# A two-layer hybrid attention and MLP trunk on one core: attention's matmuls in a fixed order, q and k stacked by transfers, weight loads on another queue

## The chip, the core and the metric

The kernel runs on one core of one Trainium2 chip. Its matrix engine (TensorE, PE in the profile) multiplies; VectorE (DVE) and ScalarE (ACT) do elementwise work; GpSimd (POOL) does little here; SyncE (SP) issues transfers. The time is the device time of one execution in microseconds (us), smaller is better; a kernel's time is the median over its runs.

## The reference

Sequence 512, width 1024, two layers, all in float32. Each layer has an attention part and a gated MLP part, both conditioned on a vector c by modulations (scale, shift, gate). The attention has sixteen heads in three groups: four heads A (differential attention: two score maps per head, rotary), six heads B (a mixture of dilated windows, rotary), six heads C (a data-dependent bias from cumulative log-forget gates).

```python
h = rmsnorm(x) * (1 + scale1(c)) + shift1(c)
qa, ka, va, qb, kb, vb, qc, kc, vc, fz = split(h @ w_in)
oa = softmax(qa1 ka1') va - lam * softmax(qa2 ka2') va      # A, rotary q and k
ob = dilated-window mixture over rotary qb, kb, vb          # B
oc = softmax(qc kc' + cum[q] - cum[k]) vc                   # C, cum = cumsum(log_sigmoid(fz + bias))
x = x + gate1(c) * (concat(oa, ob, oc) @ w_out)
x = x + gate2(c) * MLP(rmsnorm(x) * (1 + scale2(c)) + shift2(c))
```

## The kernel before

Products keep float32's precision by splitting each operand into a high and a low part of a type that PE multiplies in one pass; one product is three matmuls (hi by hi, low by hi, hi by low), issued by mm3 (L250 to L253). A weight tile arrives by a 512 KB load (L148, tile raww, three buffers), ACT makes its high part (L174, whi), DVE the low part (L186, wlo). Modulations are also loaded by 512 KB tiles (L214, rawm, two buffers) and reduced on DVE (L217); they are spread over the attention loops and the MLP.

A framework builds the program: it takes the operations in the order in which the code issues them as a priority and sets for each engine an order of its own, with waits between the engines; an operation may be passed by a later one of its engine that the framework expects to be ready sooner. issue_after keeps one operation behind another.

layer_attn (L366) works on eight head pairs, ORDER = B0 B1 A0 C0 A1 C1 B2 C2, indexed 0 to 7. Each pair has eight blocks: two heads by four blocks of 128 queries; the n-th query block sees the first 128 n keys. The loop at L806 runs over all 64 blocks. For block b it issues the scores of the next block (emit_S, L611: tile s in PSUM), the masked row maximum on DVE (L641), the exponential on ACT (L654), and for the block two back (lag = 2) the transposes (L682, tile pt), the high part on ACT (L701, pth), the low part on DVE (L706, ptl) and the product with V (emit_PV, L728 and L729, tile po). Between these steps fill (L590) spends a budget on other PE work of the pair: the next pair's q and k projections (qk_chunk, L494: 24 matmuls a side into a PSUM tile qkps), then half of a group of V products (v_half, L388: 48 matmuls of 256 columns, tile vps), and for the last pair the first output products (out_part, tile ops).

A projection is followed by qk_post (L446), one step at a time between blocks. For A and B: ACT copies the PSUM tile (L456), two transfers swap even and odd rows (L458, L459, on SP), DVE applies the rotary tables (L462, L464, L466). Then the operands of the scores are laid out so that one 128-row matmul holds two of the three split products:

- B and C: stack_gen (L416) builds stacked tiles qk from half-height (64-row) steps: high part on ACT (L423), low part on DVE (L420), copies on ACT (L434, L436). For C it reads the projection's PSUM tile itself, which stays occupied so long.
- A: one high and one low part (split_gen, L240 and L242), then twelve transfers of 32 rows for each side (L477).
- C gets its bias as four extra rows (L443), which come from fz_post (L508): a chain of small DVE operations on z, two sums on PE (pf, L536 and L537), transposes (pa, L559).

PSUM has eight banks: three of the pool mm (projections, V and output products), two for s, two for pt, one for po. Weight and modulation loads, swaps and layout transfers all go out on SP's queue, in one order.

Of the kernel before, what the change touches and what calls it, by code (L numbers as in the profile page):

```python
# [30 lines left out]
def kernel(  # L31
# [106 lines left out]
    class Weights:  # L138
        def __init__(self):
            self.raw, self.w = {}, {}  # L140
            self.nd = self.nh = self.nl = self.nu = 0
            self.pt = None

        def dma(self, upto):
            while self.nd < min(upto, len(plan)):
                src, n, at = plan[self.nd]
                t = rawp.tile([128, 4 * VZ], F32, tag="raw", name="raww")
                nc.sync.dma_start(out=t[:, 0:n], in_=src)  # L148
                self.raw[self.nd] = t
                self.nd += 1  # L150

# [93 lines left out]
    def pair_tiles(pool, tag, name):  # L245
        hi = pool.tile([128, SEQ], F32R, tag=tag, name=name + "h")
        lo = pool.tile([128, SEQ], F32R, tag=tag, name=name + "l")
        return hi, lo

    def mm3(ps, w, rhs, first, last, c=slice(0, SEQ)):  # L250
        T.matmul(ps[:, c], w[0], rhs[0][:, c], start=first, stop=False, skip_group_check=True)  # L251
        T.matmul(ps[:, c], w[0], rhs[1][:, c], start=False, stop=False, skip_group_check=True)  # L252
        T.matmul(ps[:, c], w[1], rhs[0][:, c], start=False, stop=last, skip_group_check=True)  # L253

    def feat_q(ps, w, act, first=True, last=True, k0=0):
        n = len(act)
# [109 lines left out]
    def layer_attn(l, ap, mods, st, rt0):  # L366
# [21 lines left out]
        def v_half(q, half):  # L388
            nb, n = (1, VZ) if q == 0 else (2, 256)
            if half == 0:  # L390
                pools = {"m": (mm, "mm"), "t": (ps_t, "pt"), "o": (ps_o, "o")}
                vps[q] = [pools[c][0].tile([128, SEQ], F32, tag=pools[c][1], name="vps")
                          for c in ("otmt" if q == 0 else "mm")]
            pss = vps[q]
            w = W.use()
            for j in range(4):
                k = 4 * half + j
                wc = w(n * j, n * j + n)
                for tb in range(4):
# [4 lines left out]
                    T.matmul(d, h[k][0][:, b], wc[0], start=go, stop=False, skip_group_check=True)  # L404
                    T.matmul(d, h[k][0][:, b], wc[1], start=False, stop=False, skip_group_check=True)
                    T.matmul(d, h[k][1][:, b], wc[0], start=False, stop=en, skip_group_check=True)
                W.pump(j)
                yield
            if half == 1:
                if q == 0:  # L410
                    for tb in range(4):
                        V.tensor_tensor(out=z[:, tb, :], in0=pss[tb][:, 256:VZ], in1=fb[:, l, :], op=ALU.add)
                vvs[q] = ap.tile([128, 4, 4, 128], F32R, tag="vv", name="vv", bufs=2)
                aux.append(v_post(q, lambda tb: pss[tb // nb][:, 256 * (tb % nb):256 * (tb % nb) + 256]))

        def stack_gen(src, side, res, pair=None):  # L416
            R = (H0, H1)

            def sub(out, h):
                V.tensor_tensor(out=out, in0=src[R[h]], in1=res[h][R[h]].bitcast(F32), op=ALU.subtract)  # L420

            for h in range(2):
                A.activation(out=res[h][R[h]], in_=src[R[h]], func=AF.Copy)  # L423
                yield
                if side == 0:
                    sub(res[h][R[1 - h]], h)
                elif pair is None:
                    sub(res[2 + h][R[h]], h)
                else:
                    sub(res[2 + h][H0], h)  # L430
                yield
                dup = res[h][R[1 - h]] if side == 1 else res[2 + h][H0] if pair is not None else None
                if dup is not None:
                    A.activation(out=dup, in_=src[R[h]], func=AF.Copy)  # L434
                if side == 1 and pair is None:
                    A.activation(out=res[2 + h][R[1 - h]], in_=res[2 + h][R[h]].bitcast(F32), func=AF.Copy)  # L436
                yield
            if pair is not None:
                while not aug:
                    yield  # L440
                for h in range(2):
                    c = 24 * side + 4 * (2 * (pair - 5) + h)
                    nc.sync.dma_start(out=res[2 + h][64:68, :].bitcast(F32), in_=aug[0][c:c + 4, :].bitcast(F32))  # L443
                yield

        def qk_post(idx, side, ps, kind):  # L446
# [1 line left out]
            res = [ap.tile([128, SEQ], F32R, tag="qk", name="qk", bufs=QKB) for _ in range(n)]  # L448
            qks[idx, side] = res
            if kind == "C":  # L450
                yield from stack_gen(ps, side, res, ORDER[idx][1])
                qkdone.add((idx, side))
                return
            tb = rope_tile(kind)
# [11 lines left out]
            V.tensor_tensor(out=qf, in0=qf, in1=sw, op=ALU.add)  # L466
            yield
            if kind != "A":
                yield from stack_gen(qf, side, res)
# [98 lines left out]
        def out_part(m):  # L568
            ops[m] = mm.tile([128, SEQ], F32, tag="mm", name="ops") if m < 3 else ps_s.tile([128, SEQ], F32, tag="s", name="ops")
            w = W.use()  # L570
            for k in range(7):
# [3 lines left out]
                W.pump(k)  # L575
                yield

        fills = []
        for idx in range(8):
            f = []  # L580
# [6 lines left out]
            cost = (10.4 if idx < 7 else 9.08) + (5.2 if idx < 6 else 0)  # L587
            fills.append([f, cost, 0.0])

        def fill(idx, share):  # L590
# [20 lines left out]
        def emit_S(b):  # L611
# [3 lines left out]
            qb = slice(128 * i, 128 * i + 128)  # L615
            if kind != "A":
                s = ps_s.tile([128, SEQ], F32, tag="s", name="s")
                T.matmul(s[:, 0:n], q[hh][:, qb], k[hh][:, 0:n], start=True, stop=False)
                if kind == "B":
                    T.matmul(s[:, 0:n], q[hh][:, qb], k[2 + hh][:, 0:n], start=False, stop=True)  # L620
                else:
                    T.matmul(s[:, 0:n], q[2 + hh][0:68, qb], k[2 + hh][0:68, 0:n], start=False, stop=True)
                S[b] = [s]
                return
            res = []
            for mp in range(2):
                s = ps_s.tile([128, SEQ], F32, tag="s", name="s")
                T.matmul(s[:, 0:n], q[2 * hh + mp][0:96, qb], k[2 * hh + mp][0:96, 0:n], start=True, stop=True)  # L628
                res.append(s)
            S[b] = res  # L630

# [41 lines left out]
        def emit_T(b):  # L673
# [5 lines left out]
                pt = ps_t.tile([128, SEQ], F32, tag="pt", name="pt")  # L679
            for j in range(i + 1):  # L680
                c = 128 * (i + j) if i < 2 else 128 * j
                T.transpose(pt[:, c:c + 128], e[:, 128 * j:128 * j + 128], ident)  # L682
# [25 lines left out]
        def emit_PV(b):  # L708
# [14 lines left out]
            for j in range(nj):  # L723
# [4 lines left out]
                T.matmul(po[:, oc], vv[:, j, hd, :], pth[:, pc], start=(j == 0), stop=False, skip_group_check=True)  # L728
                T.matmul(po[:, oc], vv[:, j, hd, :], ptl[:, pc], start=False, stop=(j == nj - 1), skip_group_check=True)  # L729
            if half == 1:  # L730
                aux.append(head_post(idx, kind, hh, po))

# [69 lines left out]

        emit_S(0)
        lag = 2
        f1, f2, f3 = 0.06, 0.055, 0.055
        for b in range(nb + lag):  # L806
            idx = blocks[min(b, nb - 1)][0]
            while idx and fills[idx - 1][0]:
                fill(idx - 1, 1.0)
            p = b - lag  # L810
# [13 lines left out]
            if p >= 0:  # L824
                emit_hi(p)
            fill(idx, f1)
            if b < nb:
                emit_exp(b)
            if p >= 0:
                emit_lo(p)  # L830
            fill(idx, f2)
            if b + 1 < nb:
# [2 lines left out]
            if b < nb:  # L835
                emit_norm(b)
            fill(idx, f3)
            if p >= 0:
# [6 lines left out]
        for idx in range(8):  # L845
            while fills[idx][0]:
                fill(idx, 1.0)
        while any(g.__name__ == "head_post" for g in aux):
# [332 lines left out]
```

## Time and profile before

| | |
|---|---|
| median of 3 runs | 1338.02 us (1337.93 to 1339.64) |
| the profiled execution | 1334.63 us |
| its span | 1332.9 us |
| PE, DVE, ACT busy in the span | 96%, 64%, 48% |
| mean granted PE clock | 0.989 |
| attention loop, first layer | about 64 to 283 us |
| attention loop, second layer | about 716 to 927 us |

The median stands 3.4 us above the profiled execution, whose time is 1.7 us longer than the span. In the profile a row names the line, the engine, the operation and the program's tiles, out<-in; busy time and the mean of one; and the idle time of the engine ahead of it with what ended it. A PE row is a matmul whose end is modelled, and rows overlap, so PE's idle time shows only gaps that are longer than that overlap.

### The profile page before, as it was taken

To read this page: it belongs to the slowest core of one execution; us is meant where nothing else is said; L and a number is where in the kernel's file an instruction comes from. 1 tells how busy PE (TensorE), PEld (TensorE's weight loads), DVE (VectorE), ACT (ScalarE), POOL (GpSimd) and SP (SyncE) were. 2 spreads that over 40 slices of the span, in tenths; PEclk is the share of its full clock that TensorE was granted. 3 is DMA by queue.
4 is the path that set the end of the run, shared out by engine and by line. 5 is a ranking of instruction groups with operands and counts; after the bars stand their busy time and mean duration, and the time that the engine had idled before them with its cause. 6 is when DMAs were issued, how large, how long until landed. Compare 5 with 4: busy or idle time off the path is not lost.

```text
span 1332.9 us, 17722 instructions
## 1 busy us (share of the span) xinstructions
PE 1277.8 (96%) x6568; PEld 1058.6 (79%) x6568; DVE 858.2 (64%) x1600; ACT 642.3 (48%) x1158; POOL 22.9 (2%) x16
## 2 busy tenths in 40 slices
PE   4899999999999999999999999999999999999997
PEld 1788888788877778888898888878878888888886
DVE  6888999868888874423347788875754444443232
ACT  5576677745333243322336677785543333333231
POOL 5100000000000000000000000000000000000000
PEclk8899999999999999999999999999999999999999
DMA  9345454433888853332432334212133333332331
GB/s 373 140 141 183 152 180 136 130 110 129 269 261 266 267 173 95 91 103 87 117 110 95 90 103 141 66 56 90 48 109 96 97 95 95 95 91 87 103 99 63
DMA packets 56601, 174.39 MB, mean 131 GB/s; under 512 B 8130, under 2 KB 10450, under 8 KB 56516
## 3 DMA queue, kind: packets, MB, share of 16 engines
q1 hardware_dynamic: 55364, 172.16, 41.0%
q8 instruction: 52, 0.85, 0.3%
q10 hardware_dynamic: 1088, 1.05, 0.2%
q14 instruction: 33, 0.27, 0.1%
q0 software_dynamic: 64, 0.06, 0.0%
HBM read 159.41 MB, written 2.10 MB: 121 GB/s over the span
## 4 chain that ended last, share of the span: by engine, by line
PE 53%; DMA 8%; DVE 7%; ACT 4%; issue 3%; SPq 0%; DVEq 0%; ACTq 0%
DMA rawm<-in_wmod_dram 7%; PE dps L251 6%; PE dps L253 6%; PE dps L252 6%; PE pu L251 4%; PE pu L253 4%; PE pu L252 4%; PE pg L252 4%; PE pg L253 4%; PE pg L251 4%; DVE wlo L186 1%; DVE rawm L217 1%; PE qkps L251 1%; PE qkps L252 1%; PE qkps L253 1%
## 5 line engine op out<-in xcount | busy, mean ns | idle before, releaser
L186 DVE TENSOR_TENSOR wlo<-raww,whi 128x1024 fp32r<-128x1024 f32 (+3 forms) x188 | 224.2, 1193 | 241.0 <-ACT whi L174 236.5
L174 ACT ACTIVATE whi<-raww 128x1024 fp32r<-128x1024 f32 (+3 forms) x188 | 194.5, 1035 | 329.6 <-PE dps L252 137.7
L253 PE MATMUL pu<-hh,wlo 128*128 128x512 f32 (+1 forms) x368 | 141.2, 384 | 3.5 <-DVE wlo L186 3.5
L252 PE MATMUL pg<-hl,whi 128*128 128x512 f32 (+1 forms) x368 | 143.0, 389 | 1.5 <-DVE hl L300 1.5
L251 PE MATMUL pg<-hh,whi 128*128 128x512 f32 (+1 forms) x368 | 141.6, 385 | 1.6 <-ACT whi L174 1.6
L251 PE MATMUL pu<-hh,whi 128*128 128x512 f32 (+1 forms) x368 | 142.4, 387 | 0.5 <-ACT whi L174 0.5
L253 PE MATMUL pg<-hh,wlo 128*128 128x512 f32 (+1 forms) x368 | 140.9, 383 | 1.1 <-DVE wlo L186 1.1
L252 PE MATMUL pu<-hl,whi 128*128 128x512 f32 (+1 forms) x368 | 140.7, 382 | 0.0
L251 PE MATMUL dps<-mh,whi 128*128 128x512 f32 x308 | 121.5, 395 | 0.0
L253 PE MATMUL dps<-mh,wlo 128*128 128x512 f32 x308 | 121.5, 394 | 0.0
L252 PE MATMUL dps<-ml,whi 128*128 128x512 f32 x308 | 121.2, 393 | 0.0
L217 DVE CUSTOM_DVE_ANT_0 rawm<-rawm,scb,bm 128x1024 f32<-128x1024 f32 x80 | 102.3, 1279 | 23.7 <-DMA rawm<-in_wmod_dram 23.4
L654 ACT ACTIVATE e<-e,nm 128x256 f32<-128x256 f32 (+3 forms) x160 | 89.0, 557 | 33.0 <-DVE nm L641 29.9
L251 PE MATMUL qkps<-hh,whi 128*128 128x512 f32 x224 | 95.1, 424 | 4.7 <-ACT qk L434 4.1
L898 ACT ACTIVATE y<-y 128x512 f32<-128x512 f32 x44 | 27.8, 632 | 142.6 <-DVE y L895 142.6
L252 PE MATMUL qkps<-hl,whi 128*128 128x512 f32 x224 | 89.7, 400 | 0.0
L253 PE MATMUL qkps<-hh,wlo 128*128 128x512 f32 x224 | 89.6, 400 | 0.0
L253 PEld LDWEIGHTS pu<-hh,wlo 128*128 128x128 f32 x368 | 69.1, 188 | 22.1 <-DVE wlo L186 6.9
L641 DVE CUSTOM_DVE_ANT_0 e<-s,cst 128x256 f32<-128x256 f32 (+3 forms) x160 | 76.4, 481 | 12.0 <-PE s L628 3.7
L252 PEld LDWEIGHTS pg<-hl,whi 128*128 128x128 f32 x368 | 69.0, 188 | 17.7 <-DVE hl L300 3.1
L253 PEld LDWEIGHTS pg<-hh,wlo 128*128 128x128 f32 x368 | 69.0, 188 | 16.7 <-DVE wlo L186 1.9
L251 PEld LDWEIGHTS pg<-hh,whi 128*128 128x128 f32 x368 | 69.1, 188 | 16.0 <-ACT whi L174 2.0
(176 smaller groups left out, 2663.2 us busy)
## 6 DMA issues: line engine op xcount, KB each, us to landing
raww<-in_wup_dram SPq DMA_DIRECT2D x88, 512.0 KB
rawm<-in_wmod_dram SPq DMA_DIRECT2D x80, 512.0 KB
raww<-in_wqk_dram SPq DMA_DIRECT2D x32, 512.0 KB
raww<-in_wdown_dram SPq DMA_DIRECT2D x32, 512.0 KB
mu<-in_wmod_dram SPq DMA_DIRECT2D x16, 512.0 KB
raww<-in_wout_dram SPq DMA_DIRECT2D x16, 448.0 KB
raww<-in_wv_dram SPq DMA_DIRECT2D x12, 512.0 KB
raww<-in_wdown_dram SPq DMA_DIRECT2D x16, 384.0 KB
```

The lines of the kernel that those rows point to most:

```text
L174: A.activation(out=h[:, 0:m], in_=self.raw[i][:, c:c + m], func=AF.Copy)
L186: V.tensor_tensor(out=lo[:, 0:m], in0=raw[:, c:c + m], in1=h[:, 0:m].bitcast(F32), op=ALU.subtract)
L217: V.tensor_tensor_reduce(out=raw, in0=raw, in1=scb, scale=1.0, scalar=bm[:, l, ci:ci + 1], op0=ALU.mult, op1=ALU.add, accum_out=dst)
L251: T.matmul(ps[:, c], w[0], rhs[0][:, c], start=first, stop=False, skip_group_check=True)
L252: T.matmul(ps[:, c], w[0], rhs[1][:, c], start=False, stop=False, skip_group_check=True)
L253: T.matmul(ps[:, c], w[1], rhs[0][:, c], start=False, stop=last, skip_group_check=True)
L641: anchor[0] = V.tensor_tensor_reduce(out=e[:, 0:n], in0=s[:, 0:n], in1=cst[:, mask + SEQ - n:mask + SEQ], scale=-scale, scalar=3e38, op0=A ...
L654: anchor[1] = A.activation(out=e[:, 0:n], in_=e[:, 0:n], func=AF.Exp, bias=nm, scale=-1.0, accum_out=den).ins
L898: last_silu[0] = A.activation(out=y, in_=y, func=AF.Silu).ins
```

## The change

Five edits, all for the two attention loops:

1. *Source order on PE.* Every matmul and transpose of the loop goes through a wrapper (pe, mmul) which ties it behind the one issued before it, so that PE's order is the order of the code. The tie is on from behind the first emit_S to the end of the loop. Since mm3's matmuls go through the wrapper, PE's rows of projections, V, scores and PV all stand at one line (L259).
2. *Budgets.* The shares of the fills change from 0.17 in each block to tables (near, far, 0.125) which put more of the projections into a pair's first blocks and the V products into the later ones; two pieces of output products move to pairs 6 and 7. Each block has four more turns for the steps between. PV of a block is issued one block later.
3. *Stacking.* For B and C, split_gen makes one 128-row high part (ACT) and one low part (DVE); the stacked tiles are filled by 64-row transfers on SP (128 KB each): four for B's q, eight for B's k, six for each side of C.
4. *Queue.* In the loop, weight and modulation loads go out on GpSimd's queue in place of SP's.
5. What follows from these: with them the order of the loads and of other operations around the loop moves too.

The core of the difference:

```diff
+            self.q = nc.sync
...
-                nc.sync.dma_start(out=t[:, 0:n], in_=src)
+                self.q.dma_start(out=t[:, 0:n], in_=src)
...
-        nc.sync.dma_start(out=raw, in_=wmod[l, ci])
+        W.q.dma_start(out=raw, in_=wmod[l, ci])
...
+    row = [False, None]
+
+    def pe(ins):
+        with (tc.issue_after(row[1]) if row[0] and row[1] else ExitStack()):
+            r = ins()
+        row[1] = r.ins
+
+    def mmul(*a, **k):
+        pe(lambda: T.matmul(*a, **k))
...
-        def stack_gen(src, side, res, pair=None):
+        def stack_gen(src, hi, lo, side, res, pair=None):
             R = (H0, H1)
-
-            def sub(out, h):
-                V.tensor_tensor(out=out, in0=src[R[h]], in1=res[h][R[h]].bitcast(F32), op=ALU.subtract)
-
+            yield from split_gen(src, hi, lo)
             for h in range(2):
-                A.activation(out=res[h][R[h]], in_=src[R[h]], func=AF.Copy)
-                yield
                 if side == 0:
-                    sub(res[h][R[1 - h]], h)
-                elif pair is None:
-                    sub(res[2 + h][R[h]], h)
+                    cp = [(h, R[h], hi), (h, R[1 - h], lo)] + ([(2 + h, H0, hi)] if pair is not None else [])
                 else:
-                    sub(res[2 + h][H0], h)
-                yield
-                dup = res[h][R[1 - h]] if side == 1 else res[2 + h][H0] if pair is not None else None
-                if dup is not None:
-                    A.activation(out=dup, in_=src[R[h]], func=AF.Copy)
-                if side == 1 and pair is None:
-                    A.activation(out=res[2 + h][R[1 - h]], in_=res[2 + h][R[h]].bitcast(F32), func=AF.Copy)
+                    cp = [(h, H0, hi), (h, H1, hi), (2 + h, H0, lo)] + ([(2 + h, H1, lo)] if pair is None else [])
+                for j, rows, t in cp:
+                    nc.sync.dma_start(out=res[j][rows, :].bitcast(F32), in_=t[R[h], :].bitcast(F32))
                 yield
...
+        near = [0.155, 0.155, 0.15, 0.15, 0.12, 0.1, 0.085, 0.085]
...
+            if idx == 6:
+                f += [part(outs[0], 6)]
             if idx == 7:
-                f += [out_part(m) for m in range(nout)]
+                f += [part(outs[1], 6)] + outs[0:3]
...
         emit_S(0)
         lag = 2
-        f1, f2, f3 = 0.06, 0.055, 0.055
-        for b in range(nb + lag):
+        row[0] = True
+        W.q = G
+        for b in range(nb + lag + 1):
             idx = blocks[min(b, nb - 1)][0]
+            f1 = f2 = f3 = share[idx][b % 8] / 3 if b < nb else 0.0
+            for _ in range(4):
+                tick()
...
-            if p >= 0:
-                emit_PV(p)
+            if p >= 1:
+                emit_PV(p - 1)
...
+        row[0] = False
+        W.q = nc.sync
```

Three places show how instructions move. First PE, at the start of the first layer's loop, where the last V products (vps) of the stretch before meet the first scores (s); qkps are projections of the next pair. Before:

```order
L406 MATMUL vps<-whi,hl 128x262
L251 MATMUL qkps<-hh,whi 128x512
L252 MATMUL qkps<-hl,whi 128x512
L253 MATMUL qkps<-hh,wlo 128x512
L618 MATMUL s<-qk 128x128
```

And now:

```order
L259 MATMUL vps<-wlo,hh 128x262
L259 MATMUL vps<-whi,hl 128x262
L259 MATMUL s<-qk 128x128 x2
L259 MATMUL qkps<-hh,whi 128x512
L259 MATMUL qkps<-hl,whi 128x512
```

The first block's two score matmuls stand straight behind the V products, ahead of all projections of the next pair. At the start of the second layer's loop it is the same; there fifteen projections stood ahead of the first score matmul before.

Second SP's queue, from the loads ahead of the transfers of A0 (qk filled 32 rows at a time) on. Before:

```order
L458 DMA sw<-qf 64x512
L459 DMA sw<-qf 64x512
L214 DMA rawm<-in_wmod_dram 128x1024
L148 DMA raww<-in_wv_dram 128x1024
L214 DMA rawm<-in_wmod_dram 128x1024
L477 DMA qk<-sw 32x512 x2
L458 DMA sw<-qf 64x512
```

And now, behind the transfers of the B pair ahead of it:

```order
L436 DMA qk<-sw 64x512 x2
L436 DMA qk<-qf 64x512 x2
L459 DMA sw<-qf 64x512
L460 DMA sw<-qf 64x512
L478 DMA qk<-sw 32x512 x2
L478 DMA qk<-qf 32x512
```

The loads are gone from between; the stacking transfers (L436) have come in.

Third GpSimd's queue at the program's start, where bm and gA are small loads, the products on mu belong to the first modulations, and au is a tile of C's bias. Before:

```order
L989 DMA bm<-in_bmod_dram 128x96
L989 DMA gA<-in_gattn_dram 128x16
L1036 ISA
L1036 TENSOR_TENSOR mu<-mu,scb 128x1024 x8
L550 MEMSET au 128x192 x2
```

And now:

```order
L1009 DMA gA<-in_gattn_dram 128x16
L215 DMA rawm<-in_wmod_dram 128x1024
L1056 ISA
L1056 TENSOR_TENSOR mu<-mu,scb 128x1024
L551 MEMSET au 128x192
L1056 TENSOR_TENSOR mu<-mu,scb 128x1024 x7
L149 DMA raww<-in_wv_dram 128x1024
```

One modulation load goes out ahead of the products, a memset has moved between them, and the weight loads follow behind them.

More of the change, by code (lines that the diff above doesn't have):

```diff
@@ L248, in pair_tiles @@
         return hi, lo
+    row = [False, None]
[5 more added lines that the diff above has]
+        pe(lambda: T.matmul(*a, **k))
     def mm3(ps, w, rhs, first, last, c=slice(0, SEQ)):
-        T.matmul(ps[:, c], w[0], rhs[0][:, c], start=first, stop=False, skip_group_check=True)
-        T.matmul(ps[:, c], w[0], rhs[1][:, c], start=False, stop=False, skip_group_check=True)
-        T.matmul(ps[:, c], w[1], rhs[0][:, c], start=False, stop=last, skip_group_check=True)
+        mmul(ps[:, c], w[0], rhs[0][:, c], start=first, stop=False, skip_group_check=True)
+        mmul(ps[:, c], w[0], rhs[1][:, c], start=False, stop=False, skip_group_check=True)
+        mmul(ps[:, c], w[1], rhs[0][:, c], start=False, stop=last, skip_group_check=True)
     def feat_q(ps, w, act, first=True, last=True, k0=0):
@@ L403, in v_half @@
                     en = k == KC - 1
-                    T.matmul(d, h[k][0][:, b], wc[0], start=go, stop=False, skip_group_check=True)
-                    T.matmul(d, h[k][0][:, b], wc[1], start=False, stop=False, skip_group_check=True)
-                    T.matmul(d, h[k][1][:, b], wc[0], start=False, stop=en, skip_group_check=True)
+                    mmul(d, h[k][0][:, b], wc[0], start=go, stop=False, skip_group_check=True)
+                    mmul(d, h[k][0][:, b], wc[1], start=False, stop=False, skip_group_check=True)
+                    mmul(d, h[k][1][:, b], wc[0], start=False, stop=en, skip_group_check=True)
                 W.pump(j)
@@ L450, in qk_post @@
             if kind == "C":
-                yield from stack_gen(ps, side, res, ORDER[idx][1])
+                hi, lo = (tmp(nm, "rp").bitcast(F32R) for nm in ("ch", "cl"))
+                yield from stack_gen(ps, hi, lo, side, res, ORDER[idx][1])
                 qkdone.add((idx, side))
@@ L468, in qk_post @@
             if kind != "A":
-                yield from stack_gen(qf, side, res)
+                yield from stack_gen(qf, sw.bitcast(F32R), qf.bitcast(F32R), side, res)
             else:
@@ L576, in out_part, with part @@
                 yield
+        def part(g, n):
+            for _ in range(n):
+                next(g)
+                yield
+        outs = [out_part(m) for m in range(nout)]
+        near = [0.155, 0.155, 0.15, 0.15, 0.12, 0.1, 0.085, 0.085]
+        far = [0.18, 0.18, 0.17, 0.15, 0.09, 0.08, 0.075, 0.075]
+        share = [far if idx < 7 and ORDER[idx + 1][0] == "A" else [0.125] * 8 if idx == 7 else near for idx in range(8)]
         fills = []
@@ L584, in layer_attn @@
                 f += [v_half(idx // 2 + 1, idx % 2)]
+            if idx == 6:
+                f += [part(outs[0], 6)]
             if idx == 7:
-                f += [out_part(m) for m in range(nout)]
-            cost = (10.4 if idx < 7 else 9.08) + (5.2 if idx < 6 else 0)
+                f += [part(outs[1], 6)] + outs[0:3]
+            cost = (10.4, 9.75)[idx // 7] + (5.2 if idx < 6 else 3.9 if idx == 6 else 0)
             fills.append([f, cost, 0.0])
@@ L617, in emit_S @@
                 s = ps_s.tile([128, SEQ], F32, tag="s", name="s")
-                T.matmul(s[:, 0:n], q[hh][:, qb], k[hh][:, 0:n], start=True, stop=False)
+                mmul(s[:, 0:n], q[hh][:, qb], k[hh][:, 0:n], start=True, stop=False)
                 if kind == "B":
-                    T.matmul(s[:, 0:n], q[hh][:, qb], k[2 + hh][:, 0:n], start=False, stop=True)
+                    mmul(s[:, 0:n], q[hh][:, qb], k[2 + hh][:, 0:n], start=False, stop=True)
                 else:
-                    T.matmul(s[:, 0:n], q[2 + hh][0:68, qb], k[2 + hh][0:68, 0:n], start=False, stop=True)
+                    mmul(s[:, 0:n], q[2 + hh][0:68, qb], k[2 + hh][0:68, 0:n], start=False, stop=True)
                 S[b] = [s]
@@ L627, in emit_S @@
                 s = ps_s.tile([128, SEQ], F32, tag="s", name="s")
-                T.matmul(s[:, 0:n], q[2 * hh + mp][0:96, qb], k[2 * hh + mp][0:96, 0:n], start=True, stop=True)
+                mmul(s[:, 0:n], q[2 * hh + mp][0:96, qb], k[2 * hh + mp][0:96, 0:n], start=True, stop=True)
                 res.append(s)
@@ L727, in emit_PV @@
                 pc = slice(a, a + 256 - c0)
-                T.matmul(po[:, oc], vv[:, j, hd, :], pth[:, pc], start=(j == 0), stop=False, skip_group_check=True)
-                T.matmul(po[:, oc], vv[:, j, hd, :], ptl[:, pc], start=False, stop=(j == nj - 1), skip_group_check=True)
+                mmul(po[:, oc], vv[:, j, hd, :], pth[:, pc], start=(j == 0), stop=False, skip_group_check=True)
+                mmul(po[:, oc], vv[:, j, hd, :], ptl[:, pc], start=False, stop=(j == nj - 1), skip_group_check=True)
             if half == 1:
```

10 lines of the change are left out of this document (6 added, 4 removed).

## The prediction

> **What bounds the kernel now.** I read the page's busy shares first, then a table of stages, then what TensorE's idle time in the two attention loops waited for.
>
> ```profile
> span 1332.9 us, 17722 instructions
> PE 1277.8 (96%) x6568; PEld 1058.6 (79%) x6568; DVE 858.2 (64%) x1600; ACT 642.3 (48%) x1158; POOL 22.9 (2%) x16
> ```
>
> TensorE (PE) is busy for 96% of the span, so an edit counts by what it does to the time between PE's matmuls. The change touches the two attention loops, 64 to 283 us and 716 to 927 us, and the stretch before each. The table of stages for the loops, then two pieces of the first loop and one piece of the second MLP (columns: stretch, length, busy us and instructions of each engine, PE's granted clock, DMA share, GB/s):
>
> ```profile
> 64.00:283.00 219.00, 211.19 (x1257) 178.91 (x1256) 194.69 (x475) 157.84 (x351) 0.00 (x0) 0.99 0.49 152
> 716.00:927.00 211.00, 206.62 (x1244) 174.37 (x1243) 166.40 (x414) 155.30 (x346) 0.00 (x0) 1.00 0.30 91
> ...
> 120.00:160.00 40.00, 37.61 (x217) 31.89 (x216) 37.63 (x102) 28.76 (x69) 0.00 (x0) 0.96 0.56 175
> 160.00:200.00 40.00, 37.82 (x247) 32.85 (x245) 37.86 (x95) 30.36 (x69) 0.00 (x0) 1.00 0.55 172
> ...
> 1100.00:1140.00 40.00, 40.00 (x175) 32.51 (x174) 18.40 (x22) 14.94 (x19) 0.00 (x0) 1.00 0.30 92
> ```
>
> PE shows 219.0 - 211.2 = 7.8 us idle in the first loop and 4.4 in the second: 12.2 us that anybody can see. Beside it DVE is 94% busy in the two pieces of the first loop (37.63 and 37.86 of 40). But a busy PE is not PE at its peak. The MLP piece gives the pace of a row without waits: 40.00 us / 175 = 229 ns for each 512-column matmul. I price the first loop's list at such a pace. The groups of PE in the first loop, a stretch of V products alone, and four transposes with the matmul behind them:
>
> ```profile
> L251 PE MATMUL qkps<-hh,whi 128*128 128x512 f32 x112 | 47.2, 421 | 4.3 <-ACT qk L434 4.1
> L682 PE MATMUL pt<-cst,e 128*128 128x128 f32 x160 | 29.4, 279 | 0.1
> L404 PE MATMUL vps<-whi,hh 128*128 128x256 f32 x96 | 28.2, 297 | 0.0
> L728 PE MATMUL po<-pth,vv 128*128 128x256 f32 x96 | 24.7, 275 | 0.9 <-ACT pth L701 0.6
> L251 PE MATMUL ops<-oh,whi 128*128 128x512 f32 x31 | 13.3, 429 | 0.2 <-ACT oh L240 0.2
> ```
> ```profile
> 706.00:712.00 6.00, 6.00 (x51) 6.00 (x51) 0.00 (x0) 0.00 (x0) 1.00 0.33 94
> ```
> ```profile
> 811.96 0.60 PE L682 MATMUL pt<-cst,e 128*128 128x128 f32 x4
> 812.31 0.37 PE L404 MATMUL vps<-whi,hh 128*128 128x256 f32 x1
> ```
>
> Projections and output products: 3 x (112 + 31) = 429 at 229 ns, 98 us. V products: 3 x 96 at 118 ns (6.00 / 51), 34 us. PV: 192, a third of them half as wide, 19 us. Scores: 128 of 320 columns on average (128 to 512), 18 us by columns. Transposes: 160 at 0.1 us (0.35 us for four rounded up), 16 us. The rest, about 6. Sum 191 us. The first loop's 219 less 7.8 idle and some 1.6 lost to a slow clock (below) leave 18 us that no idle column shows; the second loop's 206.6 leave 16. They are short gaps where one kind of matmul follows another, and waits that a pipelined matmul hides.
>
> The waits of PE with names, in the first loop and in the second:
>
> ```profile
> PE qkps L251 <- ACT qk L434: 4.1, 2, 2.1
> ...
> PE pf L537 <- DVE z L529: 0.4, 1, 0.4
> ```
> ```profile
> PE s L618 <- DVE nm L641: 0.9, 1, 0.9
> PE pt L682 <- ACT e L654: 0.8, 3, 0.4
> ```
> ```profile
> 139.73 0.30 PE L682 MATMUL pt<-cst,e 128*128 128x128 f32 x1
> 142.14 0.66 PE L251 MATMUL qkps<-hh,whi 128*128 128x512 f32 x1 [2.11 <-ACT qk L434]
> ```
>
> Only one wait is of size: twice a projection waited 2.1 us for a PSUM buffer that stack_gen of a C pair (L434 copies out of it) still held. Each cost 2.1 us, and after the first the clock of that piece is 0.96 over 40 us, which is 3.2 us at half speed, 1.6 lost.
>
> **The change part by part.**
>
> *Stacking by transfers: what goes.* C's projection is left after one ACT and one DVE step instead of six half-height steps, so both 2.1-us waits go: -4.1, and -1.6 with the clock: **-5.7**. Over a loop's three C and two B pairs ACT does 30 steps fewer and DVE 10 (by the code); off PE's path, but it shortens what other waits stand behind. Of the other visible idle, 3.7 us in the first loop and 4.4 in the second, I take **-5** (0 to -8.1).
>
> *Source order, later PV.* The order listing has fewer places where PE passes from one kind of matmul to another: 279 and 281 in the loops, 340 and 315 before. That alone is a sixth and a tenth of the hidden 18 and 16 us, -5. PV of a block now runs one block later than its hi and lo parts, and its 256-column row above shows waits for those (pth). I take a good third of the hidden 34 us: **-12** (-5 to -18).
>
> *The start of each loop.* Here PE loses. The order before lets 3 and 15 projections run ahead of the first scores; the fixed order puts the scores straight behind the V products. The second loop's start, PE, then DVE, ACT and SP:
>
> ```profile
> 712.56 0.28 PE L406 MATMUL vps<-whi,hl 128*128 128x262 f32 x1
> ...
> 716.22 0.50 PE L618 MATMUL s<-qk 128*128 128x128 f32 x2
> ```
> ```profile
> 709.47 1.22 DVE L186 TENSOR_TENSOR wlo<-raww,whi 128x1024 fp32r<-128x1024 f32 x1 [4.56 <-ACT whi L174]
> ...
> 713.02 1.28 DVE L466 TENSOR_TENSOR qf<-qf,sw 128x512 f32<-128x512 f32 x2
> ```
> ```profile
> L242 DVE TENSOR_TENSOR qf<-qf,sw 128x512 fp32r<-128x512 f32 x4 | 2.7, 685 | 0.8 <-ACT sw L240 0.8
> L240 ACT ACTIVATE sw<-qf 128x512 fp32r<-128x512 f32 x4 | 2.5, 626 | 1.0 <-DVE qf L466 1.0
> ```
> ```profile
> L477 SPq DMA_DIRECT2D qk<-sw x64: 507/588/1625, 108.1 to 823.6; - x64
> ```
> ```profile
> 56.74 0.60 SPq L459 DMA_DIRECT2D sw<-qf  x1
> ```
> ```profile
> 58.15 0.69 DVE L462 TENSOR_TENSOR qf<-qf,rope 128x512 f32<-128x512 f32 x1 [4.37 <-DMA sw<-qf]
> ```
>
> PE is free at 712.68 (the V product's start and 0.12). q's rope ends at 713.66 and k's at 714.30. Behind them the split: q's high part (ACT 0.63) at 714.29, its low part (DVE 0.685, behind k's rope) at 714.99, k's at 714.93 and 715.68. The first block's scores need six transfers, two of q and four of k, in SP's order at 0.59 us an issue (L477 is the nearest row): 714.3 to 714.9, 715.0 to 715.6, and four more to 718.0. The last swap of the first layer was issued by 57.34 and DVE could start at 58.15, 0.8 us to land: 718.8. So 6.1 us idle, less 0.3 that PE loses before 716.22 today: **+5.8**. In the first layer:
>
> ```profile
> 63.80 0.28 PE L406 MATMUL vps<-whi,hl 128*128 128x262 f32 x1
> ...
> 64.62 0.22 PE L618 MATMUL s<-qk 128*128 128x128 f32 x1
> ```
> ```profile
> 62.12 0.69 DVE L466 TENSOR_TENSOR qf<-qf,sw 128x512 f32<-128x512 f32 x1
> ```
>
> PE is free at 63.92; k's rope ends at 62.81, the parts at 63.44 and 64.12 (65.3 if a 1.22-us weight step goes first), four issues from 63.44 to 65.8, landed 66.6: **+2.7** (to 4). Clock: of the two 2.1-us waits above the first brought half speed (0.96), the second, in the next piece, did not (1.00); I count one slow window for the long gap, **+1.6** (to +3.2). The Trainium skill (TensorE: Matmul & The Clock Gate, Part 1: The HAM clock gate) says that the clock halves after an idle window of about 3.4 us; this case's 2.11-us gap did it with less, so the trace disagrees on the length. By the page's rule only the second layer's gap would count, by the row either may.
>
> *Pair boundaries.* From k's last projection matmul to the next pair's first score the fixed order leaves 48 V products, two to four blocks' worth of scores, transposes and PV: 8.6 to 9.5 us at the paces above (6.2 for the last pair, C2). The chain for B is copy out of PSUM 0.63 (as L240), two swaps 1.2, landing 0.8, two rope steps at 0.685 (as L242) 1.37, split 1.31, four issues 2.4, landing 0.8: 8.5 us; for A with six issues 9.7; for C 5.1. So B and C are covered and A is short by 1, if no step stands in a queue. DVE is 94% busy in the first loop, so steps do stand behind others of 0.7 to 1.3 us. Bounds: 0 (the cover holds everywhere) and +18 (each of four A boundaries 2.5, each of four B boundaries 1.5, C2 1 in each layer). I take **+6**, nearest to the chain without queues plus half a microsecond at each.
>
> *The gate sums pf, pa.* They stand in PE's row behind block 5 and wait for the z chain on DVE (0.4 us today); nothing may pass them: **+1** (0 to +4).
>
> *Loads on GpSimd's queue.* The startup's stretches, GpSimd's own load, and SP's largest waits:
>
> ```profile
> 10.00:20.00 10.00, 5.35 (x7) 2.35 (x8) 5.67 (x9) 7.42 (x12) 2.17 (x2) 1.00 1.02 410
> 20.00:30.00 10.00, 3.39 (x8) 1.67 (x7) 10.00 (x10) 4.66 (x8) 10.00 (x4) 0.64 1.03 410
> ```
> ```profile
> bm<-in_bmod_dram POOLq DMA_DIRECT2D x1, 48.0 KB, 4.1
> ```
> ```profile
> SPq L148 <- DVE wlo L186: 699.3, 163, 16.0
> ...
> SPq L458 <- ACT qf L456: 57.9, 12, 14.0
> ```
>
> Loads no longer stand between swaps and transfers on SP, where one could wait up to 16.0 us for its buffer; that is what makes the boundary's chain as short as counted, so I count it once, there. In the loops nothing is late: three weight buffers and two modulation buffers run ahead, and 4.1 us to landing is less than one modulation's interval (24 of them in the 219 us, 9 us). 0 (-1 to +5). But one modulation load needs no buffer and so goes out at the very start, into a stretch where the DMA engines are full at 410 GB/s: 512 KB, **+1.3** (0 to 2.3, with GpSimd's memset that moved between its eight products there).
>
> *Sum.* -5.7 - 5 - 12 + 5.8 + 2.7 + 1.6 + 6 + 1 + 1.3 = -4.3. The profiled execution took 1334.6 us (1332.9 of span, 1.7 around it), so 1330.3; its median stands 3.4 us above it (1338.0), so **1334** as a median.
>
> **The rivals.**
>
> *The boundaries end late (slower).* In a fixed row nothing may run ahead of a pair's first score. If steps queue on DVE and ACT as in the upper bound, the boundaries cost 18 instead of 6 and the gate sums 4: -4.3 + 12 + 3 = +11, 1349. From 0.3 us more at each of the 14 boundaries the gain is gone, from 0.5 it is a loss. For it: DVE at 94%; the cover and chain of B within 1 us of each other. Against: ACT and DVE have 40 steps fewer in each loop, and in the second loop DVE is at 79% (166.4 of 211).
>
> *PE's waits were the queue's (faster by more).* If half of the hidden 34 us and all visible idle go, and the boundaries cost 2: -4.3 - 5 - 3 - 4 = -16, 1322. For it: the many short waits for pth and nm; against: gaps at a change of kind stay whatever the order.
>
> *Loads starve on GpSimd's queue (slower).* If GpSimd can't hand out a load while DVE works, loads drift later until DVE itself waits for a modulation: 24 in the first loop and 0.6 us each are +14, 1348. The Trainium skill (SBUF — State Buffer, SBUF: two separate sides) states such a lock for DVE operations in a two-port mode. In the trace GpSimd's products ran beside a DVE at 10.00 of 10 and were 10.00 of 10 busy themselves, which speaks against a lock by this kernel's operations, if not for descriptors.
>
> *The parts cancel.* Starts and boundaries eat what the waits give: 1338. A difference below 0.2%, 2.7 us, is no change by what a measurement of this kernel can tell.
>
> **How the numbers follow.** Forecast 1334 (1328 to 1335.3 within its case): 0.33. Faster by more: 0.17. Cancelled: 0.14. Late boundaries: 0.30. Starved loads: 0.06. Faster 0.33 + 0.17 = 0.50, same 0.14, slower 0.36. The range leaves out a tenth at each end: 1320 (a little beyond the faster rival) to 1351 (beyond the late boundaries).
>
> **What would show it.** Right: no wait of a projection for a C pair's copy; an idle PE of 5 to 6 us before the second loop's first score and about 3 before the first's; a first loop of some 208 us behind that gap (219 - 5.7 - 2 - 6 + 3) and a second of 205 (211 - 3 - 6 + 3), DVE in the first loop some 7 us less busy. Wrong: PE waiting for transfers (qk) at most boundaries; DVE waiting for rawm or PE for whi in the loops; loops that are longer although each named wait is gone, which would refute the hidden third.

## The result and the profile after

The changed kernel takes 1465.9 us (median of 4 runs, 1460.9 to 1466.7); the one before 1338.5 in the runs beside it. The ratio is 1.0947, with a 95% interval of 1.0928 to 1.0967: slower by 127 us. The prediction said 1334 and at most 1351.

The page of the changed kernel, its first lines and the clock line of its 40 slices:

```profile
span 1459.1 us, 17992 instructions
## 1 busy us (share of the span) xinstructions
PE 1304.8 (89%) x6568; PEld 1084.3 (74%) x6568; DVE 849.3 (58%) x1576; ACT 601.5 (41%) x1086; POOL 60.2 (4%) x86
...
PEclk8889989899999999999998989899999999999999
```

PE has as many matmuls as before, yet its share fell from 96% to 89% and the busy time itself rose by 27 us. DVE and ACT are less busy, as the edit of the stacking had it, and gained nothing by it: PE waited. The two loops, each from the last V product ahead of it to its last PV product; before, then after (columns as in the prediction):

```profile
64.00:278.00 214.00, 206.19 (x1234) 174.80 (x1233) 191.84 (x471) 154.91 (x347) 0.00 (x0) 0.99 0.50 153
713.00:922.00 209.00, 204.62 (x1233) 172.65 (x1232) 166.32 (x418) 155.25 (x347) 0.00 (x0) 1.00 0.30 92
```
```profile
65.00:345.00 280.00, 220.52 (x1232) 188.04 (x1231) 187.98 (x460) 134.92 (x311) 23.92 (x45) 0.89 0.55 150
779.00:1048.00 269.00, 216.96 (x1235) 185.76 (x1234) 163.08 (x407) 135.54 (x311) 11.18 (x21) 0.90 0.41 108
```

The same 1230 matmuls take 549 us in place of 423: the whole loss is here. Read each row as two differences. Length less busy time is idle time: 59.5 and 52.0 us now, 7.8 and 4.4 before, 99 more. The busy time of the same work is 437.5 in place of 410.8, 27 more: that is the clock. It is 0.89 and 0.90 on the mean; by the trace's clock records 61 and 51 us ran at half speed, and half of the busy time in them, 19 and 17 us, was lost beyond the idle time (1.7 and 0 before). Take idle and clock loss away and 201 and 200 us are left, where the kernel before has 204.5 and 204.6. So the changed kernel did close short gaps, by 8 us over both layers, and paid 99 in idle time and 34 in clock for it: 125 of the 127.

Who PE waited for:

```profile
PE s L259 <- DMA qk<-qf: 45.3, 11, 10.0
PE s L259 <- DMA qk<-sw: 21.0, 7, 6.0
...
PE qkps L259 <- ACT qf L457: 8.6, 6, 1.7
...
PE s L259 <- DMA qk<-aT: 8.1, 3, 4.1
PE pf L538 <- DVE z L530: 7.5, 2, 4.6
```

No projection waits for a C pair's copies any more, as forecast; six now wait for the copy that empties a B or A projection's bank (qf). The bulk is first scores of a pair that wait for transfers into qk, 77 us with one of 2.2 us on cl that is not shown; they wait at the majority of pair boundaries, which is what the prediction named as its sign of being wrong. The longest, at A0 in the second layer: PE, then SP's queue, then DVE and ACT.

```profile
850.28 0.28 PE L259 MATMUL vps<-whi,hl 128*128 128x256 f32 x1
860.51 0.45 PE L259 MATMUL s<-qk 96*128 96x128 f32 x1 [9.95 <-DMA qk<-qf]
```
```profile
839.27 1.20 SPq L478 DMA_DIRECT2D qk<-sw  x2
...
846.75 0.51 SPq L478 DMA_DIRECT2D qk<-qf  x1
847.32 0.58 SPq L478 DMA_DIRECT2D qk<-sw  x1
848.00 0.53 SPq L459 DMA_DIRECT2D sw<-qf  x1
848.57 0.60 SPq L460 DMA_DIRECT2D sw<-qf  x1
855.78 1.19 SPq L478 DMA_DIRECT2D qk<-sw  x2
...
859.15 0.58 SPq L478 DMA_DIRECT2D qk<-qf  x1
```
```profile
843.17 0.59 ACT L457 ACTIVATE qf<-qkps 128x512 f32<-128x512 f32 x1
```
```profile
852.07 0.68 DVE L463 TENSOR_TENSOR qf<-qf,rope 128x512 f32<-128x512 f32 x1
...
855.78 0.69 DVE L243 TENSOR_TENSOR qf<-qf,sw 128x512 fp32r<-128x512 f32 x1
```

k's copy is done at 843.76, but its swaps go out at 848.00: all twelve transfers of q stand ahead of them on SP, 0.5 to 1 us each, and five of them are still to go out when the copy is done. 4.2 us are gone there. The swaps are issued by 849.17, the rotary step begins at 852.07, behind other steps of DVE, the split ends at 856.5, and the sixth transfer's issue ends at 859.73. The V products that were to cover all this ended at 850.56. The chain from the copy's start is 17 us where the prediction had 9.7.

### The profile page after: what moved, and what is told of

Read it like the earlier page. It is cut to its first block, busy times and chain, and to the rows that moved or that the text cites. A ratio compares the mean times of both kernels' runs of the same rounds, so it can differ in the third digit from the quotient of the medians.

```text
span 1459.1 us, 17992 instructions
## 1 busy us (share of the span) xinstructions
PE 1304.8 (89%) x6568; PEld 1084.3 (74%) x6568; DVE 849.3 (58%) x1576; ACT 601.5 (41%) x1086; POOL 60.2 (4%) x86
## 4 chain that ended last, share of the span: by engine, by line
PE 54%; DMA 9%; DVE 5%; issue 3%; ACT 2%; SPq 1%; DVEq 0%; ACTq 0%
PE dps L259 16%; PE pu L259 12%; PE pg L259 12%; DMA rawm<-in_wmod_dram 6%; PE qkps L259 6%; PE ops L259 3%; PE vps L259 1%; PE s L259 1%; DVE rawm L218 1%; PE pt L694 1%; DMA qk<-qf 1%; PE po L259 1%; DMA qk<-aT 1%; DVE wlo L187 1%; DMA sw<-qf 0%
## 5 line engine op out<-in xcount | busy, mean ns | idle before, releaser
L259 PE MATMUL pg<-hl,whi 128*128 128x512 f32 (+1 forms) x368 | 143.0, 389 | 1.5 <-DVE hl L311 1.5
L259 PE MATMUL pu<-hh,wlo 128*128 128x512 f32 (+1 forms) x368 | 141.2, 384 | 3.0 <-DVE wlo L187 2.9
L259 PE MATMUL s<-qk 128*128 128x128 f32 (+11 forms) x256 | 70.3, 346 | 81.8 <-DMA qk<-qf 45.3
L259 PE MATMUL pg<-hh,whi 128*128 128x512 f32 (+1 forms) x368 | 141.5, 385 | 1.6 <-ACT whi L175 1.6
L259 PE MATMUL pu<-hh,whi 128*128 128x512 f32 (+1 forms) x368 | 142.4, 387 | 0.2 <-ACT whi L175 0.2
L259 PE MATMUL pg<-hh,wlo 128*128 128x512 f32 (+1 forms) x368 | 141.0, 383 | 1.1 <-DVE wlo L187 1.1
L259 PE MATMUL pu<-hl,whi 128*128 128x512 f32 (+1 forms) x368 | 140.7, 382 | 0.0
L259 PE MATMUL dps<-mh,whi 128*128 128x512 f32 x308 | 121.5, 394 | 0.0
L259 PE MATMUL dps<-mh,wlo 128*128 128x512 f32 x308 | 121.5, 394 | 0.0
L259 PE MATMUL dps<-ml,whi 128*128 128x512 f32 x308 | 121.2, 393 | 0.0
L259 PEld LDWEIGHTS s<-qk 128*128 128x128 f32 (+2 forms) x256 | 49.3, 205 | 94.1 <-issue 34.0
L259 PE MATMUL qkps<-hh,whi 128*128 128x512 f32 x224 | 101.8, 455 | 8.6 <-ACT qf L457 8.6
L259 PE MATMUL qkps<-hl,whi 128*128 128x512 f32 x224 | 94.2, 420 | 0.0
L259 PE MATMUL qkps<-hh,wlo 128*128 128x512 f32 x224 | 93.3, 416 | 0.0
L259 PEld LDWEIGHTS pu<-hh,wlo 128*128 128x128 f32 x368 | 69.1, 188 | 21.6 <-DVE wlo L187 6.4
L259 PEld LDWEIGHTS pg<-hl,whi 128*128 128x128 f32 x368 | 69.0, 188 | 17.6 <-DVE hl L311 3.1
```

Of the source, the lines that this page charges most:

```text
L259: pe(lambda: T.matmul(*a, **k))
```

## The experiments

Theory 1: the fixed order. A wait that other matmuls used to fill now stands open, and the low clock comes with it. Theory 2: the stacking transfers are slow by themselves. Theory 3: loads on GpSimd's queue are late. Where an interval stands, the ratio is to the kernel before in the same set of runs; the others are single timings beside it. A difference between two sets is uncertain by some microseconds: the kernel before had medians from 1335.0 to 1338.5 in them, and the changed kernel's four executions spread from 1460.9 to 1466.7.

**The changed kernel untied.**

```diff
-        row[0] = True
```

> The changed kernel without the tie between matmuls: PE's order is the framework's again; budgets, stacking by transfers, later PV and GpSimd's loads stay. Theory 1, the fixed order: PE waits at the first scores of a pair because nothing may pass them while q's and k's steps and transfers end late; untied, other matmuls fill that time, the waits for transfers (about 75 us by name) go below 10 us in total, the clock returns to about 0.985, and the time lies between 1330 and 1350. Theory 2, the stacking: transfers land too late whatever the order, PE still waits for them, and the time stays above 1400. Theory 3, GpSimd's loads starve: above 1400 too, with PE or DVE waiting for weights.

1376.6 us, ratio 1.0295 (1.0270 to 1.0320). It is 41 us slower than the kernel before it was timed with, so 86 of the 127 us are the order's; waits of first scores for transfers fall from 77 us to 18, and the clock's mean is 0.975. Theory 1 has the larger part, but 41 us stay, above its range: something else costs too.

**The kernel before, tied.**

```diff
+        row[0] = True
```
(with the wrappers pe and mmul around its matmuls)

> The kernel before with the tie alone: its budgets, its stacking by half-height steps, its PV and its queue for loads stay. Theory 1: the swaps and A's transfers alone are late at the boundaries, and loads stand between them on SP: 1390 to 1450, waits of the first scores of A pairs of 8 us or more each. Theory 2: without the stacking transfers little is late: 1338 to 1355.

1427.6 us, 92 above the kernel before. No stacking transfer, no new queue, no new budget, and nearly three quarters of the loss. Its loops and its largest waits inside them:

```profile
64.00:324.00 260.00, 223.63 (x1234) 190.31 (x1233) 195.47 (x468) 156.23 (x346) 0.00 (x0) 0.89 0.40 126
759.00:1015.00 256.00, 222.64 (x1239) 189.95 (x1238) 170.74 (x419) 157.10 (x348) 0.00 (x0) 0.91 0.25 75
```
```profile
PE s L258 <- DVE nm L651: 11.7, 10, 2.8
PE s L258 <- DMA qk<-qf: 11.2, 5, 5.6
PE s L258 <- ACT qk L444: 10.0, 5, 3.4
...
PE po L258 <- DVE ptl L716: 7.5, 12, 1.3
```

Waits of 1 to 5 us for every kind of step: maxima, copies, transfers, low parts. PE is idle for 70 us (516 less 446.3), 57 more than before, and its busy time rose by 35 us, from 410.8 to 446.3. By the clock records 42 us were lost to the low clock, 40 more than before. What is left without both is 202 and 203 us, so the tie alone closed 4 us of short gaps. The range was right; that A pairs alone would carry it with 8 us each was not, the longest wait is 5.6.

**The changed kernel with the stacking of before.**

```diff
-            yield from split_gen(src, hi, lo)
+                A.activation(out=res[h][R[h]], in_=src[R[h]], func=AF.Copy)
...
```

> The changed kernel with the stacking by half-height steps of before; the tie, the budgets, later PV and GpSimd's loads stay. Theory 1: the A boundaries keep their four waits of about 10 us and a slow clock behind each, those of B and C and the two starts shrink: 1395 to 1425. Theory 2: 1335 to 1355.

1438.3 us, 28 less than the changed kernel, 13 above theory 1's range. The waits at A0 and A1 stay (10.0, 9.4, 6.4 and 6.0 us), as theory 1 had it, and pf waits 7.4 us in the first layer, which I had not counted.

**Swaps on another queue.**

```diff
-            nc.sync.dma_start(out=sw[0::2, :], in_=qf[1::2, :])
+            nc.scalar.dma_start(out=sw[0::2, :], in_=qf[1::2, :])
```
(and the second one)

> The changed kernel with the two swap transfers of each rotary projection issued on ACT's queue in place of SP's, so that k's swaps no longer stand behind q's transfers. If SP's issue in turn makes the chain long (4.2 us from k's copy to its swap at A0 in the second layer), the four A waits shrink by about 4 us each and the B waits by 1 to 2, the time falls by 20 to 35 us to 1430 to 1445. If the time from issue to landing is what is long, it falls by less than 8 us, or rises with ACT's issues.

1442.9 us, 23 less: SP's order of issue is a part, as expected. But the wait at A0 in the second layer falls only from 9.95 to 7.16 us, not by 4: the swap now goes out among q's transfers, by 833.99, and DVE can use it at 839.55, 5.6 us later.

**GpSimd's queue alone, on the kernel before.**

```diff
+        W.q = G
```

> The kernel before with one part of the change alone: weight and modulation loads of the loops on GpSimd's queue. Theory 3 (loads starve there): 1350 or more, with DVE waiting for rawm or PE for whi inside the loops. Otherwise (theories 1 and 2): 1330 to 1341, since swaps no longer stand behind loads on SP.

1354.6 us, ratio 1.0141 (1.0122 to 1.0159): 19.5 us slower. In the loops DVE waits for a load once, for 0.6 us, and PE never; the mechanism of theory 3 is not there, its cost is. PE's idle time in the loops rises from 12 to 23 us, and its clock loss from 2 to 10. DVE waits for swaps instead:

```profile
DVE qf L463 <- DMA sw<-qf: 19.7, 11, 3.7
```
```profile
115.46 0.53 POOL L149 DMA_DIRECT2D raww<-in_wqk_dram  x1 [3.89 <-DVE wlo L187]
```
```profile
116.92 0.60 SPq L460 DMA_DIRECT2D sw<-qf  x1
```
```profile
122.39 0.69 DVE L463 TENSOR_TENSOR qf<-qf,rope 128x512 f32<-128x512 f32 x1 [3.69 <-DMA sw<-qf]
```
```profile
DMA to landing us min/median/max: 2.0/3.3/4.6
```

The last row is of the second swap (L460). Before, DVE waited 6.4 us for swaps. A 512 KB load leaves GpSimd at 115.46, the swap SP at 116.92 to 117.52, and DVE can go on at 122.39, 4.9 us later. The trace's packets show the load's moving from 117.0 to 120.2; SP's queue moves none from 116.7 to 118.5, and its packets then run between the load's. With all of it in one queue such a load stands ahead of the swap or behind it. That the swaps are late beside such loads is what the trace shows; why SP's packets pause is not shown.

**Stacking by transfers alone, on the kernel before.**

```diff
+            yield from split_gen(src, hi, lo)
...
+                for j, rows, t in cp:
+                    nc.sync.dma_start(out=res[j][rows, :].bitcast(F32), in_=t[R[h], :].bitcast(F32))
```

> The kernel before with one part alone: B's and C's stacking by transfers, in the framework's own order and with loads still on SP. The untied changed kernel kept 41 us of the loss. If the stacking transfers carry that: 1360 to 1385, with waits of first scores for qk transfers and with swaps and loads queueing behind sixteen more issues a pair on SP. If budgets and later PV carry it: 1330 to 1345.

1323.6 us, ratio 0.9918 (0.9895 to 0.9941): 11.4 us faster than the kernel before, the fastest of all. The edit is the change's stack_gen and its two calls, nothing else. Its loops:

```profile
64.00:271.00 207.00, 201.92 (x1228) 172.59 (x1227) 183.59 (x456) 133.63 (x311) 0.00 (x0) 1.00 0.69 206
705.00:909.00 204.00, 202.40 (x1232) 173.71 (x1230) 157.31 (x406) 133.34 (x311) 0.00 (x0) 0.99 0.50 140
```

411 us in place of 423; idle 5.1 and 1.6 us in place of 7.8 and 4.4, no wait for C's bank. I had expected either a loss or nothing; theory 2 falls: where other matmuls may run ahead, the longer chain is hidden, and there are some 50 steps fewer on ACT and DVE in each loop (36 and 12 to 15 by the rows). Without idle time and clock loss 202 and 201 us are left, with no fixed order: the stacking alone closed 6 to 7 us of short gaps. That this comes from the fewer steps was not tried.

**Filler matmuls ahead of the first scores.**

```diff
+            def pad(s):
+                for _ in range({0: 10, 2: 30, 4: 30, 6: 16}.get(idx, 0) if b % 8 == 0 else 0):
+                    mmul(s, h[0][0][:, 0:128], h[0][0], start=True, stop=True, skip_group_check=True)
```

> The changed kernel with matmuls added that compute nothing of use, tied in PE's row ahead of a pair's first scores: 30 of 512 columns at A0 and A1, 16 at B2, 10 at each loop's start, so 7, 3.7 and 2.3 us of work at full clock inside waits of 10, 6 and 6 us; their result is overwritten by the scores. If PE's idleness is what lowers the clock, and the low clock is a part of the loss of its own (36 us by a count of slow stretches), slow stretches at these places get shorter and the time falls, by 8 to 20 us, to 1445 to 1458, although PE has 40 us of work more. If the low clock has another cause or is hidden by the waits, the time stays at 1466 or rises.

1458.1 us with 172 matmuls more, 39 us of work: 7.9 less than the changed kernel's median, 2.9 less than its profiled execution (1460.9).

```profile
65.00:345.00 280.00, 238.19 (x1323) 202.54 (x1322) 189.17 (x460) 135.85 (x314) 23.82 (x45) 0.93 0.55 151
779.00:1045.00 266.00, 232.18 (x1317) 198.50 (x1316) 162.54 (x406) 135.63 (x311) 11.13 (x21) 0.95 0.41 109
```

The clock is 0.93 and 0.95 in place of 0.89 and 0.90; busy time rose by 32.9 (470.4 less 437.5), less than the 39 of the filler, because the clock loss fell from 36.0 to 29.5 us. So idleness does lower the clock, and the low clock costs time of its own. The gain itself is at the edge of what I expected and not clear of the scatter; what is clear is that 39 us of useless work cost nothing. The filler sat at four places in each loop, and the others stayed.

**First scores alone untied.**

```diff
+            sm1 = T.matmul if b % 8 == 0 else mmul
```
(used in emit_S; everything else stays tied)

> The changed kernel in which the score matmuls of each pair's first block alone are outside the tie (all others stay in source order). If the loss of the fixed order sits at the pairs' first scores, others can run ahead of them there and most of the 89 us that the untied kernel won back come back here too: 1380 to 1415. If the order costs at many places, 1430 or more.

1439.4 us, 26.5 less, not 50 to 86. In the new order only about a dozen matmuls pass such a score (three transposes and up to nine of a projection, some 2.5 us of work); waits of 9.1 us for transfers stay, and 58 of the 77 us of such waits. So the run left most of the waits at first scores in place and can't tell whether the loss sits there. That a fixed order opens waits at many places is what the tie alone shows, above.

**Budgets and later PV alone, on the kernel before.** (The tables of shares, the output products' places, four turns more a block, PV one block later.)

```diff
+            f1 = f2 = f3 = share[idx][b % 8] / 3 if b < nb else 0.0
+            for _ in range(4):
+                tick()
...
+            if p >= 1:
+                emit_PV(p - 1)
```

> The kernel before with one part alone: the tables of shares, output products of pairs 6 and 7 moved, four more turns a block, PV one block later; untied, stacking by half-height steps, loads on SP. If the parts add up, the untied changed kernel's +41 less GpSimd's +19.5 plus the stacking's -11.4 leave +33 for this part: 1360 to 1375. If instead the parts harm each other (swaps that collide with loads from GpSimd's queue and with sixteen stacking transfers a pair), this part alone is near nothing: 1330 to 1345.

1356.1 us, ratio 1.0155 (1.0127 to 1.0182), 19.5 slower. In its loops PE is idle 22 us in place of 12 and at a mean clock of 0.96 and 0.98; among its waits are projections for C's bank (4.5 us, 4 times) and PV for pth (3.3, 5 times). Between the two ranges: it costs, but less than the rest of a sum. Which of its four pieces does it was not tried.

**The changed kernel with loads on SP.**

```diff
-        W.q = G
```

> The changed kernel with its loads back on SP's queue; the tie, budgets, later PV and stacking by transfers stay. If GpSimd's loads cost by collisions with swaps and stacking transfers, the time falls by 15 to 30: 1436 to 1451. If loads on SP hold up the swaps and transfers of a fixed row (a load waits there up to 19 us for its buffer), it rises: 1475 to 1520.

1436.5 us, 29 less (28 by the kernels before of the two sets). GpSimd's queue costs in the tied kernel too, by these single timings more than alone. This pair differs by the queue alone, and the landing of the stacking transfers (L436) shows it; loads on GpSimd's queue, then on SP's:

```profile
DMA to landing us min/median/max: 2.3/5.4/7.2
```
```profile
DMA to landing us min/median/max: 2.2/2.3/4.5
```

**Stacking with budgets, untied, loads on SP.** (The two edits tried alone above, together.)

```diff
-        row[0] = True
-        W.q = G
```
(against the changed kernel)

> The kernel before with stacking by transfers, and with budgets and later PV; untied, loads on SP. If the parts add up (-11 and what the budgets alone cost): 1345 to 1365. If the budgets cost only where loads are on GpSimd's queue: 1318 to 1330.

1336.0 us, ratio 0.9999 (0.9984 to 1.0013): no change that can be told from none, between the two ranges. A sum of the two would have been +8; PE's waits for C's bank, 4.5 us with the budgets alone, are gone here.

**The tie with stacking by transfers.** (On the kernel before; its budgets, PV and queue stay.)

```diff
+        row[0] = True
...
+            yield from split_gen(src, hi, lo)
```

> The kernel before with the tie and with stacking by transfers; its own budgets, PV and queue stay. The tie alone gave 1428, the stacking alone 1324. If the parts only add, the stacking takes its 11 to 13 us off: 1412 to 1420. If the stacking's longer chain (issues, landing) is hidden in a free row and stands open in a fixed one, it adds instead: 1435 to 1465.

1435.1 us, 97 above the kernel before it was timed with, where the tie alone was 92 above its own; at the lower edge of the second range. The same stacking that gains 11 in a free row gains nothing in a fixed one and rather loses 5, where first scores wait 44 us for its and A's transfers (qk<-qf and qk<-sw). This is one timing against one; in the loops of the two traces PE is idle 82 us against 70.

**What follows.** The parts alone, each on the kernel before, are +92 (tie), +19.5 (GpSimd's queue), +19.5 (budgets and later PV) and -11.4 (stacking): 120 of the measured 127. That the sum comes so near is in part luck, for the parts don't simply add: without the tie the other three are 28 in sum and 41 together, budgets and stacking are 8 in sum and nothing together, and the stacking's gain is gone under the tie. That the tie is the largest part stands without the sum: 92 alone, 86 taken out of the whole.

## Why the prediction was wrong

The forecast was a gain of 4 us; the kernel lost 127. The step that failed is how the fixed order was priced: waits were taken over from a trace in which other matmuls fill them, with +6 for all pair boundaries and +1.6 for the clock. The tie alone cost 92: idle time rose from 12 to 70 us and clock loss from 2 to 42. Step by step, by the terms of the sum:

- *C's bank* (-5.7): right. Those waits are gone, here and with the stacking alone.
- *Other visible idle* (-5, bounds 0 to -8.1): wrong, and wrongly bounded. I took away waits of a scheduler that could fill them and let them vanish in one that can't. The tie alone raised idle time from 12 to 70 us.
- *Hidden gaps* (-12, bounds -5 to -18): within its bounds at 8 us, but for the source order the reason was only half right. The tie alone closed 4, and the stacking alone, in a free row, 6 to 7.
- *Starts of the loops* (+5.8 and +2.7): right for the second, too low for the first. The second loop's scores waited 5.98 us and then 0.85; the first's 2.83 and then 3.60, 6.4 in all where at most 4 was allowed. With loads on SP the second wait at the first loop's start is 0.28 us and the two are 4.6 in all, so GpSimd's queue may be a part of that miss.

```profile
785.32 0.45 PE L259 MATMUL s<-qk 128*128 128x128 f32 x1 [5.98 <-DMA qk<-sw]
```
```profile
68.16 0.30 PE L259 MATMUL s<-qk 128*128 128x128 f32 x1 [2.83 <-DMA qk<-sw]
```

- *Pair boundaries* (+6, bounds 0 to +18): this term failed by the most. Of the 76.6 us that first scores waited for transfers, 13.3 are the starts; the boundaries took 63. The chain was priced as if k's steps met an empty queue on SP and nearly empty ones on DVE and ACT. In SP's order q's twelve transfers stand ahead of k's swaps, where two did before; their 0.59 us was in a row that I quoted, but I counted k's issues only. The upper bound stretched DVE's queue alone.
- *The clock* (+1.6, bound +3.2): the second term that failed. I counted a slow window for the gap at a start and none at a boundary or for the waits of every block; it was 34 us. The Trainium skill (TensorE: Matmul & The Clock Gate, Part 1: The HAM clock gate) has the clock fall after an idle window of about 3.4 us. The traces don't show that length: PE waits of 1.92 and 1.03 us within 3.3 us, with one matmul between them, were followed by a slow stretch:

```profile
820.92 0.30 PE L259 MATMUL s<-qk 128*128 128x128 f32 x1 [1.92 <-DMA qk<-sw]
822.25 0.30 PE L259 MATMUL s<-qk 128*128 128x128 f32 x1 [1.03 <-DMA qk<-qf]
```
```profile
823.56:826.97 3.41, 3.41 (x11) 2.75 (x10) 0.91 (x3) 0.30 (x2) 0.00 (x0) 0.50 0.52 181
```

- *pf and pa* (+1, bounds 0 to +4): too low, above its bound: pf waited 7.5 us, 4.6 of it in the first layer.
- *GpSimd's queue* (0, bounds -1 to +5): failed. +19.5 alone. The argument looked only at whether a load is in time for its user, not at what it does to a small transfer of another queue that DVE waits for. The rival of starved loads had the sign and nearly the size, with a mechanism that the trace doesn't show: one wait of 0.6 us for a load in the loops.
- *Startup* (+1.3): right; the first loop's start moved from 63.9 to 65.2 us.
- *Budgets and later PV* were priced as a cost nowhere, only as cover; alone they cost 19.5 us.

The rival of late boundaries had the sign and the place; its price, +11, was of steps that queue on DVE and ACT, without SP's order, the open waits of every block, the clock or GpSimd's queue.

## What to carry to other kernels

A matmul order that is fixed by hand takes away the slack that a scheduler finds: price each wait in the old trace as if nothing may pass it, not as it stands there filled, and count for each chain every instruction that its queue holds ahead of it, whichever operand it is for. In these loops the added idle time of PE was paid 1.3 times (changed kernel: 99 us and 34 of clock) to 1.7 times (tie alone: 57 and 40), once as idle time and again in a halved clock. Time the parts of a change apart: here one of four, the stacking, was worth 0.8% and lay hidden under the other three.

## What the runs showed of the hardware

- The clock falls to half in stretches of 3.41 us or multiples of it (3.41, 6.83, 10.24, 13.65 in the changed kernel's records), 113 us of them in its two loops; two waits of 1.92 and 1.03 us within 3.3 us were enough for one.
- Small transfers on SP's queue landed later while 512 KB loads went out on GpSimd's: the stacking transfers' median was 5.4 us against 2.3 with the loads on SP, in two kernels that differ by that alone. In the kernel before with its queue alone changed, the second swap's median was 3.3 and its longest 4.6; with the loads on SP and the stacking by transfers it was:

```profile
DMA to landing us min/median/max: 2.0/2.1/3.8
```
